# Weight sums of a seven-product feed-forward layer: from GpSimd to adding transfers and VectorE, with more blocks left at eight products

## The chip, the cores and the metric

The kernel runs on one core of a Trainium2 chip. The metric is the device time of one execution in microseconds (us), taken over several executions of the same program. The engines are named as in the profile: PE is TensorE (PEld its weight loads), DVE is VectorE, ACT is ScalarE, POOL is GpSimd, and SP is the engine whose queue issues nearly all transfers here. A transfer that POOL issues goes through the software queue; one that SP or ACT issues goes through a hardware queue.

## The reference, cut to what matters

The program computes one step of a two-layer transformer trunk for 512 latent tokens and 128 context tokens (640 columns in all) with a model width of 1024, all in float32. Layer 0 mixes with latent-attention and neighbourhood-attention heads, layer 1 with grouped-query attention. After each mixer stands a gated feed-forward layer of width 2816, and this is the part that the change touches:

```python
def swiglu(h, w_in, w_out):
    gate, up = jnp.split(h @ w_in, 2, axis=-1)
    return (jax.nn.silu(gate) * up) @ w_out
...
hp = modulate(rms_norm(xp, norm_ffn[l]), sh2_p, sc2_p)
hs = modulate(rms_norm(xs, norm_ffn[l]), sh2_s, sc2_s)
xp = xp + g2_p * swiglu(hp, w_ffn_in[l], w_ffn_out[l])
xs = xs + g2_s * swiglu(hs, w_ffn_in[l], w_ffn_out[l])
```

The shift, scale and gate vectors (sh, sc, g) of a layer are `silu(cond) @ w_mod[l] + b_mod[l]`, for two conditions. In layer 0 the last gate of layer 0 and five of the six vectors of layer 1 are still to be computed while the feed-forward layer runs; in layer 1 the last gate of layer 1.

## The kernel before, in words

**Precision.** Every float32 operand of a matmul is split into a rounded high part (ACT copies it, rounding) and a rest (one subtraction on DVE or POOL), and each product is three matmuls: high by high, high by rest, rest by high (`mm3`). Every matmul of the program is recorded at line 61, so stages are told apart by tile names.

**Input products of the feed-forward layer (`ffn`, L1026).** The width 2816 is cut into 22 blocks of 128. A block needs gate and up values: two weight tiles of 128 x 1024 (`wFI[l, fb, 0]` for gate and `[.., 1]` for up) against the activations of width 1024 and 640 columns, which are held as two halves of 320 columns. There are two ways to do a block.

- *Eight products* (`whole`, L1038; loop at L1067): gate and up, two column halves, eight slices of 128 of the width, three matmuls each, 96 matmuls of 320 columns. Only the two weight tiles have to be split (`unit`, L164). Blocks 0 and 1 of each layer go this way (`FEW = 2`, L1007).
- *Seven products* (loop at L1103, blocks 2 to 21): a Strassen-Winograd scheme over halves of the width, gate/up and column halves. It has seven products of four slices and three matmuls, 84 matmuls. Its left operands are the up tile itself (`wX`), half of the gate tile (`wW`), and four sums of halves of the two: two in `s13`, split into `wY`, two in `s24`, split into `wZ`. Before the change all four sums are made on POOL (L1117, L1118, L1121, L1122), each 128 x 512. Its right operands are four quadrants of the activations and the sums D, C, N, E of quadrants, made once per layer by `add_up` (L292); their rests for D and N are made on DVE, for C and E on POOL.

In a seven-product block PE's order is: X by quadrant 11, Y by D, the last product (W by E) of the block before, Z by N, X by 21, Z by 22, Y by C. Products that share a PSUM bank are taken out by ACT or DVE in between (`p1`, `p5`, `u1`, `g2`).

**Buffers.** Raw weight tiles come through a ring of three tiles (`rawp`, tag "raw", L159), which the up tiles, the tiles of the eight-product blocks and the modulation tiles `wm` share; the gate tiles have two of their own ("wr"). Split tiles have three places in each of two pools ("w"). `s13` and `s24` share two places ("ws"), taken in turn, so every `s13` takes the place of the `s13` before it. The outer ring has places for the results of a block (`hd`), which `hidden` (L1052) splits and sends to DRAM.

**Side work (`mod_side`, L1248).** While the blocks run, `step` feeds in the modulation product: for each 128 rows of `w_mod` one transfer of 512 KB into the raw ring and two DVE multiply-and-sum instructions (`junk`, L1265). How many after which block is written out by hand at L1285 to L1286 for layer 0 (48 tiles: 22 of them after the blocks from 5 on, one or two at a time, the rest in the output product) and at L1500 for layer 1 (8 tiles, one after each block from 2 on).

**Output product.** `wout` (L1163) loads and splits the output weights; its places alternate between the outer pools and a pool that opens when the block loop's pool closes.

**Order.** A scheduler sets the order of the instructions on each engine and of the transfers on each queue; every engine and every queue then works strictly in that order, so one that waits holds up what stands behind it. `ModS.make` (L276) makes the activation quadrants, partly on POOL (L286, L287), partly on DVE (L289, L290).

Of the kernel before, what the change touches and what calls it, by code (L numbers as in the profile page):

```python
# [18 lines left out]
P = 128  # L19
# [29 lines left out]
def body(ctx, tc, xT, vecs, crow, wm0, wm0g, wm1, wA, wNV, wNA, wMK, wMV, wOA, wGQ, wGK, wGV, wOC,  # L49
# [199 lines left out]
    class ModS:  # L249
# [26 lines left out]
        def make(self, i, rs, k):  # L276
            h, l = self.hl(k, i)
            c0, c1 = HALF[i]
            t = tp.tile([P, HT], F32, tag="u", bufs=7, name=f"{self.name}t{k}{i}")
            V.tensor_tensor(t, self.x[k][:, c0:c1], rs[:, c0:c1], ALU.mult)  # L280
            h32 = (self.left, self.right)[i][k]
            for a0, a1, c in HCOND[i]:
                self.act[k, i] = S.activation(h32[:, a0 - c0:a1 - c0], t[:, a0 - c0:a1 - c0], AF.Identity,
                                              bias=self.ml[:, self.sh + k, c:c + 1], scale=self.gsl[:, k, c:c + 1])
            if k % 2:
                G.tensor_scalar(h, h32, 1.0, 0.0, ALU.mult, ALU.add)  # L286
                G.tensor_tensor(l, h32, f(h), ALU.subtract)  # L287
            else:
                V.tensor_copy(h, h32)  # L289
                V.tensor_tensor(l, h32, f(h), ALU.subtract)  # L290

        def add_up(self, k):  # L292
            left = [self.left[j] for j in (k, k + 4)]
            b12, b22 = self.right[k], self.right[k + 4]
            n = tp.tile([P, HT], F32, tag="u", bufs=7, name=f"{self.name}n{k}")
            V.tensor_tensor(b22, b22, b12, ALU.subtract)
            V.scalar_tensor_tensor(n, b22, -1.0, left[0], ALU.mult, ALU.subtract)
            V.tensor_tensor(left[0], left[0], b12, ALU.subtract)
            V.scalar_tensor_tensor(left[1], n, -1.0, left[1], ALU.mult, ALU.subtract)
            for c, src in zip("DNCE", (left[0], n, b22, left[1])):  # L300
                t = self.sums[c][k]
                S.activation(t[:, 0:HT], src, AF.Copy)
                (V if c in "DN" else G).tensor_tensor(t[:, HT:T], src, f(t[:, 0:HT]), ALU.subtract)

    def residual(xo, xi, ps, ml, g, n, i):

# [697 lines left out]
                box["m"].make(c, nrm.rs, k)  # L1004
        return box, nxt

    FEW = 2  # L1007
    STAY = 3
    FIRST, SECOND = FO_ORDER[:9], FO_ORDER[9:]

# [15 lines left out]
    def ffn(l, x, pend, hm, nxt, side, opened):  # L1026
# [11 lines left out]
        def whole(ps, wt, k, c, first, last):  # L1038
            a, b = [w[:, k * P:k * P + P] for w in wt]
            mm3(ps[:, :HT], a, b, *hm.hl(k, c), first, last)  # L1040
# [23 lines left out]
                kept[fb] = dh, dl  # L1064

        step = None
        for fb in range(FEW):  # L1067
            pg, pu = [bank(f"fg{l}_{fb}{c}") for c in range(2)], pair(f"fu{l}_{fb}")
            g_, u_ = w1 if fb else w0
            for c in range(2):  # L1070
                for k in range(KT):
                    if fb == 0 and c == 0 and k == 3:
                        pend()
                        step = side(fk, hm.act[7, 1])
                        w1 = [after(hm.act[3 + 2 * i, 1], lambda: unit(wFI[l, 1, i], 1024, f"wgu{l}_1{i}")) for i in range(2)]
                        for j in range(4):
                            hm.add_up(j)
                    for ps, wt in ((pg, g_), (pu, u_)):
                        whole(ps[c], wt, k, c, k == 0, k == KT - 1)
            sg = tmp(f"sg{l}_{fb}")  # L1080
            for c, (c0, c1) in enumerate(HALF):
# [18 lines left out]
            step("fb", fb)  # L1100

        job = None
        for fb in range(FEW, FB):  # L1103

            ru = load(wFI[l, fb, 1], 1024, f"wu{l}_{fb}r")
            if fb == FEW:
                rg = load(wFI[l, fb, 0], 1024, f"wg{l}_{fb}r")
            else:
                rg = fp.tile([P, 1024], F32, tag="wr", bufs=2, name=f"wg{l}_{fb}r")
                nc.sync.dma_start(rg, wFI[l, fb, 0])  # L1110
# [3 lines left out]
            S.activation(wW[0], rg[:, 512:], AF.Copy)  # L1114
            V.tensor_tensor(wW[1], rg[:, 512:], f(wW[0]), ALU.subtract)
            s13 = fp.tile([P, 1024], F32, tag="ws", bufs=2, name=f"s13{l}_{fb}")
            G.tensor_tensor(s13[:, :512], rg[:, :512], rg[:, 512:], ALU.add)  # L1117
            G.tensor_tensor(s13[:, 512:], ru[:, :512], rg[:, :512], ALU.add)  # L1118
            wY = split(s13, f"wY{l}_{fb}")
            s24 = fp.tile([P, 1024], F32, tag="ws", bufs=2, name=f"s24{l}_{fb}")  # L1120
            G.tensor_tensor(s24[:, :512], s13[:, 512:], rg[:, 512:], ALU.add)  # L1121
            G.tensor_tensor(s24[:, 512:], s24[:, :512], ru[:, 512:], ALU.add)  # L1122
            wZ = split(s24, f"wZ{l}_{fb}")

            g, b5, b2 = bank(f"fg{l}_{fb}"), bank(f"fd{l}_{fb}"), bank(f"fu{l}_{fb}", "y")
# [37 lines left out]
        def wout(j0, n, tiles, name):  # L1163

            turn[0] += 1
            raw = (rawp.tile([P, 1024], F32, tag="raw", name=name + "r") if turn[0] % 2 else
                   fo.tile([P, 1024], F32, tag="raw", bufs=1, name=name + "r"))
# [3 lines left out]
            t = (wp.tile([P, 2, 1024], F32R, tag="w", bufs=3, name=name) if turn[0] % 2 else  # L1171
                 fo.tile([P, 2, 1024], F32R, tag="w", bufs=2, name=name))
# [102 lines left out]
    def x_again(n):  # L1275
# [7 lines left out]
    x, pend = mixer_out(wOA, oMs + oNs, [4, 5, 6, 7, 0, 1, 2, 3], x_again, mods[0], "oa", nxt, op[-1])  # L1283
    box2, nxt = next_mod("h10", gs[1][0], mods[1], SH1)
    side = mod_side([(0, wm0g, G2)] + [(1, wm1[j:j + 8], j) for j in (SH1, SC1, G1, SH2, SC2)],  # L1285
                    lambda kind, i: int(i > 4) + (i in (8, 11, 14, 17, 20)) if kind == "fb" else 1 + (i in (3, 5, 7)) if i < 8 else 2 + (i < 11) if i < 14 else 1)  # L1286
    x, pend = ffn(0, x, pend, box["m"], nxt, side, op)


# [368 lines left out]
```

## Time and profile before

| What | Value |
|---|---|
| Time, median of 3 runs | 1647.08 us (1644.03 to 1647.15) |
| The profiled execution: time | 1641.38 us |
| The profiled execution: span of the trace | 1639.6 us |
| TensorE clock granted, mean | 0.974 of full speed |
| Transfers | 212.65 MB, mean 130 GB/s |
| Software queue | 416 packets, 0.93 MB |

The span counts from the first to the last recorded instruction. In the profile's rows a group is given as line, engine, operation, output tile <- input tiles, shapes, and how many; buffer numbers are left out of the names, so that h01D in layer 0 is the tile of the sum D there, and h11D that of layer 1. A name in brackets after an idle time is what ended it. The first two rows of tenths in the page's second part tell which share of each fortieth of the span an engine was busy. The feed-forward layers lie at about 405 to 910 us and 1150 to 1632 us.

### The profile page before, as it was taken

What the parts mean: (1) busy time and instruction counts of PE and PEld (TensorE: products, weight loads), DVE (VectorE), ACT (ScalarE), POOL (GpSimd) and SP (SyncE); (2) the same over time, 40 slices, a digit from 0 to 9 for tenths busy, and PEclk for the clock granted to TensorE, in tenths of its full rate; (3) what the DMA queues carried; (4) which work ended last, traced back from release to release, by engine and by line L of the source; (5) the groups of instructions that cost most, each with busy time, mean ns of one, the idle gap of its engine ahead of it and who ended that gap; (6) DMA issues with size and microseconds to landing.
All of it is one profiled execution on the core that took longest, in us unless ns stands there. A gap on an engine that the chain in (4) does not pass through costs nothing.

```text
span 1639.6 us, 25446 instructions
## 1 busy us (share of the span) xinstructions
PE 1512.3 (92%) x9808; PEld 1434.6 (87%) x9808; DVE 1153.3 (70%) x1921; ACT 742.9 (45%) x1418; POOL 555.0 (34%) x498
## 2 busy tenths in 40 slices
PE   5999979999979888899999999999879999999997
PEld 3888858889868888889999989989868899999997
DVE  5656666875978898894895787784789867753333
ACT  4436566763544444342122556673544455541221
POOL 1225524522565455530000443222465555410000
PEclk9999979999979999999999999999999999999998
DMA  9334430004144544448863220002144443448311
GB/s 351 100 101 150 167 112 27 27 29 139 39 148 152 177 169 144 164 158 299 284 225 123 72 71 27 27 27 79 37 151 167 160 151 126 148 151 303 96 49 65
DMA packets 72970, 212.65 MB, mean 130 GB/s; under 512 B 8096, under 2 KB 12976, under 8 KB 72592
## 3 DMA queue, kind: packets, MB, share of 16 engines
q1 hardware_dynamic: 70080, 204.78, 36.7%
q10 hardware_dynamic: 2352, 5.31, 1.0%
q8 instruction: 77, 1.26, 0.3%
q0 software_dynamic: 416, 0.93, 0.2%
q14 instruction: 45, 0.37, 0.1%
HBM read 182.53 MB, written 28.46 MB: 129 GB/s over the span
## 4 chain that ended last, share of the span: by engine, by line
PE 56%; DVE 21%; DMA 10%; ACT 6%; issue 5%; POOL 2%; SPq 0%; ACTq 0%; DVEq 0%; POOLq 0%
PE fo L61 9%; PE fg L61 8%; DVE junk L1265 4%; DMA wm<-in_wm 4%; PE fd L61 3%; PE gq L61 2%; DMA wm<-in_wm0g 2%; DVE sg L1098 2%; PE nk L61 2%; PE nq L61 2%; PE fu L61 2%; DVE wX L1035 2%; PE mod L61 2%; PE go L61 1%; PE fo_2a L61 1%
## 5 line engine op out<-in xcount | busy, mean ns | idle before, releaser
L1265 DVE SCALAR_TENSOR_TENSOR junk<-wm,cb 128x1024 bf16<-128x1024 f32 x112 | 168.6, 1505 | 37.1 <-DMA wm<-in_wm 22.5
L1098 DVE TENSOR_TENSOR sg<-up,sg 128x640 f32<-128x640 f32 x40 | 62.1, 1553 | 49.0 <-ACT sg L1097 49.0
L61 PE MATMUL fg<-h01C,wY 128*128 128x320 f32 x240 | 43.7, 335 | 27.3 <-ACT u L1135 27.3
L61 PE MATMUL gq<-h10h,wgq 128*128 128x320 f32 x256 | 65.7, 315 | 0.2
L61 PEld LDWEIGHTS fg<-h01C,wY 128*128 128x128 f32 x240 | 38.5, 203 | 31.1 <-ACT u L1135 31.0
L244 POOL TENSOR_SCALAR h10h<-h10t,gs,mods 128x320 fp32r<-128x320 f32 x4 | 3.5, 876 | 182.8 <-DVE h10t L238 181.1
L1035 DVE TENSOR_TENSOR wY<-s,wY 128x1024 fp32r<-128x1024 f32 x40 | 60.3, 1507 | 1.8 <-ACT wY L1034 0.8
L1035 DVE TENSOR_TENSOR wZ<-s,wZ 128x1024 fp32r<-128x1024 f32 x40 | 50.5, 1263 | 7.6 <-ACT wZ L1034 7.6
L1034 ACT ACTIVATE wY<-s 128x1024 fp32r<-128x1024 f32 x40 | 42.4, 1059 | 22.5 <-PE fg L61 19.6
L1034 ACT ACTIVATE wZ<-s 128x1024 fp32r<-128x1024 f32 x40 | 42.1, 1053 | 20.0 <-PE fd L61 10.3
L61 PE MATMUL fg<-h11C,wY 128*128 128x320 f32 x240 | 41.2, 323 | 6.2 <-ACT u L1135 6.2
L61 PEld LDWEIGHTS gq<-h10h,wgq 128*128 128x128 f32 x256 | 44.7, 188 | 1.6 <-PE gtp L65 1.0
L61 PE MATMUL fg<-h01N,wZ 128*128 128x320 f32 x240 | 40.9, 322 | 5.4 <-ACT p L1129 5.4
L61 PE MATMUL fg<-h11N,wZ 128*128 128x320 f32 x240 | 40.1, 317 | 5.8 <-ACT p L1129 5.8
L61 PEld LDWEIGHTS fg<-h11C,wY 128*128 128x128 f32 x240 | 37.8, 197 | 7.4 <-ACT u L1135 7.4
L309 DVE SCALAR_TENSOR_TENSOR xr<-fo,mods,xr 128x320 f32<-128x320 f32 (+2 forms) x48 | 19.6, 436 | 35.0 <-PE fo L61 34.9
L61 PE MATMUL fd<-h01D,wY 128*128 128x320 f32 x240 | 40.0, 316 | 4.5 <-DVE wY L1035 4.5
L61 PE MATMUL fd<-h11D,wY 128*128 128x320 f32 x240 | 39.9, 316 | 4.5 <-DVE wY L1035 4.5
L61 PEld LDWEIGHTS fg<-h01N,wZ 128*128 128x128 f32 x240 | 37.9, 197 | 6.0 <-ACT p L1129 6.0
L61 PEld LDWEIGHTS fg<-h11N,wZ 128*128 128x128 f32 x240 | 37.4, 195 | 6.3 <-ACT p L1129 6.3
L61 PE MATMUL fg<-h01E,wW 128*128 128x320 f32 x240 | 39.0, 311 | 3.8 <-DVE g L1141 3.8
L61 PE MATMUL fg<-h01q,wX 128*128 128x320 f32 x240 | 41.9, 327 | 0.0
(3026 smaller groups left out, 5552.7 us busy)
## 6 DMA issues: line engine op xcount, KB each, us to landing
wm<-in_wm SPq DMA_DIRECT2D x48, 512.0 KB, 4.1
mraw<-in_wm SPq DMA_DIRECT2D x24, 512.0 KB, 3.9
mraw<-in_wm SPq DMA_DIRECT2D x8, 1024.0 KB, 15.3
wm<-in_wm0g SPq DMA_DIRECT2D x8, 512.0 KB, 4.5
x<-in_xT SPq DMA_DIRECT2D x8, 320.0 KB, 5.3
xr<-in_xT SPq DMA_DIRECT2D x8, 320.0 KB, 5.1
cb<-in_crow ACTq DMA_DIRECT2D x2, 1024.0 KB, 7.1
gt<-in_rpbp SPq DMA_DIRECT2D x8, 240.0 KB, 3.7
```

The costliest lines, as they stand in the source:

```text
L61: cls.last = nc.tensor.matmul(*a, **k)
L244: G.tensor_scalar(h[:, c0:c1], t, self.gsl[:, k, 0:1], self.ml[:, self.sh + k, 0:1], ALU.mult, ALU.add)
L309: V.scalar_tensor_tensor(xo[:, c0:c1], ps[:, c0 - o:c1 - o], ml[:, g + n, c:c + 1], xi[:, c0:c1], ALU.mult, ALU.add)
L1034: S.activation(t[:, 0, :], src, AF.Copy)
L1035: V.tensor_tensor(t[:, 1, :], src, f(t[:, 0, :]), ALU.subtract)
L1098: V.tensor_tensor(sg, up, sg, ALU.mult)
L1265: V.scalar_tensor_tensor(junk, raw, 1.0, cb[:, c, :], ALU.mult, ALU.mult, accum_out=mods[l][:, j0 + i, c:c + 1])
```

## The change

Five things change together.

- `FEW` becomes a pair: in layer 0 the first nine blocks, in layer 1 the first four keep eight products. Their weights from block 2 on are split by `unit` into the outer pool's three places.
- The sums: `s13` is filled by an SP transfer that reads the first half of the gate tile from DRAM twice, and then by two adding transfers of 128 x 512 that POOL issues, which add the second half of the gate tile and the first half of the up tile. The sums of `s24` go to DVE.
- The activations: for the second column half the rounding goes from POOL and DVE to ACT and all rests to DVE; all rests in `add_up` go to DVE, and the four calls of `add_up` stand behind blocks 0 and 1 (two each) instead of inside block 0.
- The side work of layer 0: none after blocks 0 to 2, then 3, 4, 3, 4, 3, 4 tiles after blocks 3 to 8, one after every third block from 9 on (five), then one after each of the first eight steps of the output product and two after the others.
- The first output weights (those over two tiles) always take the outer pools' places.

```diff
@@ ModS.make and add_up
-            if k % 2:
+            if i == 1:
+                S.activation(h, h32, AF.Copy)
+                V.tensor_tensor(l, h32, f(h), ALU.subtract)
+            elif k % 2:
...
-                (V if c in "DN" else G).tensor_tensor(t[:, HT:T], src, f(t[:, 0:HT]), ALU.subtract)
+                V.tensor_tensor(t[:, HT:T], src, f(t[:, 0:HT]), ALU.subtract)
@@ ffn
-    FEW = 2
+    FEW = 9, 4
...
+            if fb > 1:
+                g_, u_ = [unit(wFI[l, fb, i], 1024, f"wgu{l}_{fb}{i}") for i in range(2)]
+            else:
+                g_, u_ = w1 if fb else w0
...
-                        for j in range(4):
-                            hm.add_up(j)
...
+            if fb in (0, 1):
+                for j in (2 * fb, 2 * fb + 1):
+                    hm.add_up(j)
...
-            G.tensor_tensor(s13[:, :512], rg[:, :512], rg[:, 512:], ALU.add)
-            G.tensor_tensor(s13[:, 512:], ru[:, :512], rg[:, :512], ALU.add)
+            src = wFI[l, fb, 0][:, 0:512]
+            nc.sync.dma_start(s13.rearrange("p (a b) -> p a b", a=2),
+                              bass.AP(tensor=src.tensor, offset=src.offset, ap=[list(src.ap)[0], [0, 2], [1, 512]]))
+            nc.gpsimd.dma_start(s13[:, :512], wFI[l, fb, 0][:, 512:], accum_op=ALU.add)
+            nc.gpsimd.dma_start(s13[:, 512:], wFI[l, fb, 1][:, :512], accum_op=ALU.add)
...
-            G.tensor_tensor(s24[:, :512], s13[:, 512:], rg[:, 512:], ALU.add)
-            G.tensor_tensor(s24[:, 512:], s24[:, :512], ru[:, 512:], ALU.add)
+            V.tensor_tensor(s24[:, :512], s13[:, 512:], rg[:, 512:], ALU.add)
+            V.tensor_tensor(s24[:, 512:], s24[:, :512], ru[:, 512:], ALU.add)
@@ wout
+            early = len(tiles) > 1 or turn[0] % 2
@@ side work of layer 0
-                    lambda kind, i: int(i > 4) + (i in (8, 11, 14, 17, 20)) if kind == "fb" else 1 + (i in (3, 5, 7)) if i < 8 else 2 + (i < 11) if i < 14 else 1)
+                    lambda kind, i: (0, 0, 0, 3, 4, 3, 4, 3, 4)[i] if kind == "fb" and i < 9 else int(i % 3 == 0) if kind == "fb" else 1 if i < 8 else 2)
```

More of the change, by code (lines that the diff above doesn't have):

```diff
@@ L1066, in ffn @@
         step = None
-        for fb in range(FEW):
+        few = FEW[l]
+        for fb in range(few):
             pg, pu = [bank(f"fg{l}_{fb}{c}") for c in range(2)], pair(f"fu{l}_{fb}")
-            g_, u_ = w1 if fb else w0
+            if fb > 1:
+                g_, u_ = [unit(wFI[l, fb, i], 1024, f"wgu{l}_{fb}{i}") for i in range(2)]
+            else:
+                g_, u_ = w1 if fb else w0
             for c in range(2):
@@ L1102, in ffn @@
         job = None
-        for fb in range(FEW, FB):
+        for fb in range(few, FB):
             ru = load(wFI[l, fb, 1], 1024, f"wu{l}_{fb}r")
-            if fb == FEW:
+            if fb == few:
                 rg = load(wFI[l, fb, 0], 1024, f"wg{l}_{fb}r")
@@ L1165, in wout @@
             turn[0] += 1
-            raw = (rawp.tile([P, 1024], F32, tag="raw", name=name + "r") if turn[0] % 2 else
+            early = len(tiles) > 1 or turn[0] % 2
+            raw = (rawp.tile([P, 1024], F32, tag="raw", name=name + "r") if early else
                    fo.tile([P, 1024], F32, tag="raw", bufs=1, name=name + "r"))
@@ L1170, in wout @@
                               wFO[l, tiles[0]:tiles[0] + nt, :, j0 * P:(j0 + n) * P].rearrange("a p b -> p a b"))
-            t = (wp.tile([P, 2, 1024], F32R, tag="w", bufs=3, name=name) if turn[0] % 2 else
+            t = (wp.tile([P, 2, 1024], F32R, tag="w", bufs=3, name=name) if early else
                  fo.tile([P, 2, 1024], F32R, tag="w", bufs=2, name=name))
```

## The prediction

> **What bounds the kernel now.** I read the page's busy shares first, then the busy time by stretch, then PE's rows at the ends of the stretches, and last the waits of PE, DVE and the SP queue in the slow stretch.
>
> ```profile
> PE 1512.3 (92%) x9808; PEld 1434.6 (87%) x9808; DVE 1153.3 (70%) x1921; ACT 742.9 (45%) x1418; POOL 555.0 (34%) x498
> ...
> 404.70:451.50 46.80, 43.17 (x275) 40.32 (x274) 41.15 (x67) 25.84 (x53) 24.35 (x26) 1.00 0.11 34
> 451.50:754.10 302.60, 263.19 (x1670) 257.40 (x1669) 253.21 (x292) 128.25 (x207) 147.40 (x79) 0.94 0.48 163
> 1150.00:1198.20 48.20, 43.84 (x281) 41.29 (x281) 41.44 (x67) 27.96 (x55) 24.16 (x26) 1.00 0.11 33
> 1198.20:1470.80 272.60, 253.32 (x1671) 250.54 (x1670) 210.17 (x225) 131.13 (x205) 132.46 (x79) 0.97 0.44 149
> 1296.60:1469.00 172.40, 172.40 (x1178) 172.40 (x1177) 118.89 (x126) 88.52 (x138) 73.90 (x48) 1.00 0.40 137
> ```
>
> Behind each stretch stand its length, busy us of PE, PEld, DVE, ACT, POOL, the granted clock, the transfer share and GB/s. The second and fourth stretches are the twenty seven-product blocks of layers 0 and 1. The last, inside layer 1, has PE busy all through. So the same work is bound by PE late in layer 1 and by something else in layer 0, where PE idles while DVE is busy 84% of the time. The pace and the ends, from PE's rows in order of time:
>
> ```profile
> 451.52 1.92 PE L61 MATMUL fg<-h01q,wX 128*128 128x320 f32 x12
> 752.36 1.92 PE L61 MATMUL fg<-h01C,wY 128*128 128x320 f32 x12
> 1198.24 1.92 PE L61 MATMUL fg<-h11q,wX 128*128 128x320 f32 x12
> 1296.64 1.92 PE L61 MATMUL fg<-h11C,wY 128*128 128x320 f32 x12
> 1469.03 1.92 PE L61 MATMUL fg<-h11C,wY 128*128 128x320 f32 x12
> ```
>
> The last two rows are 14 blocks apart: 172.39 / 14 = 12.31 us for 84 matmuls, 0.1466 us each; twelve take 1.76. An eight-product block (96) then needs 14.07. Twenty blocks at PE's pace, to the end of the last C product, need 20 x 12.31 - 1.76 = 244.4. Layer 0 took 302.6 (752.36 + 1.76 - 451.52), layer 1 272.6: 58 and 28 us are lost. To what:
>
> ```profile
> PE fg L61 <- ACT u L1135: 27.3, 13, 3.6
> PE fg L61 <- ACT p L1129: 5.4, 2, 2.8
> PE fd L61 <- DVE wY L1035: 4.5, 1, 4.5
> ...
> DVE junk L1265 <- DMA wm<-in_wm: 19.3, 14, 3.2
> DVE junk L1265 <- DMA wm<-in_wm0g: 12.0, 7, 2.9
> ...
> SPq L161 <- DVE junk L1265: 78.0, 22, 4.5
> ...
> 551.40 2.44 PE L61 MATMUL fg<-h01C,wY 128*128 128x320 f32 x12 [3.58 <-ACT u L1135]
> 553.64 3.07 PE L61 MATMUL fg<-h01q,wX 128*128 128x320 f32 x12
> ```
>
> These are waits in layer 0's stretch (total, times, longest): PE waits for ACT's u, which stands behind DVE, which waits in order for the modulation tiles, whose transfers wait on SP until DVE frees a raw place. That is a ring of three tiles turning, 22 modulation tiles in it. After a wait of 3.58 us PE also runs slower: 551.40 to 556.55, where the next product starts, is 5.15 us instead of 3.52, that is 1.6 more.
>
> **The change, part by part.** The sum is made against the profiled execution, 1641.4 us (1639.6 of span); the median of the runs shown is 1647.1, 5.7 higher, which I add at the end.
>
> *More matmuls.* Seven blocks in layer 0 and two in layer 1 go from 84 to 96: 9 x 12 x 0.1466 = 15.8 us more PE work, all on the path. The floors become 7 x 14.07 + 13 x 12.31 - 1.76 = 256.8 in layer 0 and 2 x 14.07 + 18 x 12.31 - 1.76 = 248.0 in layer 1. Without any loss the change would gain 45.8 + 24.6 us; the rest of the working is what is lost again.
>
> *DVE and ACT rows for what follows:*
>
> ```profile
> 528.94 2.16 POOL L1122 TENSOR_TENSOR s<-s,wu_8r 128x512 f32<-128x512 f32 x1
> 529.98 2.19 DVE L1265 SCALAR_TENSOR_TENSOR junk<-wm,cb 128x1024 bf16<-128x1024 f32 x1
> 532.11 0.81 DVE L1098 TENSOR_TENSOR sg<-up,sg 128x640 f32<-128x640 f32 x1
> 532.85 0.68 DVE L1115 TENSOR_TENSOR wW<-wg_7r,wW 128x512 fp32r<-128x512 f32 x1
> 533.72 0.83 DVE L1056 TENSOR_TENSOR hd_2l<-sg,hd_2h 128x640 fp32r<-128x640 f32 x1 [0.20 <-ACT hd_2h L1055]
> 533.91 1.05 ACT L1034 ACTIVATE wX<-wu_8r 128x1024 fp32r<-128x1024 f32 x1
> 536.89 0.48 DVE L1137 TENSOR_TENSOR up<-fu,p 128x320 f32<-128x320 f32 x1
> 537.29 1.21 DVE L1265 SCALAR_TENSOR_TENSOR junk<-wm,cb 128x1024 bf16<-128x1024 f32 x1
> 541.50 1.22 DVE L1035 TENSOR_TENSOR wY<-s,wY 128x1024 fp32r<-128x1024 f32 x1
> 542.58 0.44 ACT L1097 ACTIVATE sg<-fg 128x320 f32<-128x320 f32 x1 [0.97 <-PE fg L61]
> ...
> wm<-in_wm SPq DMA_DIRECT2D x48, 512.0 KB, 4.1
> ...
> wu_2r<-in_wFI SPq DMA_DIRECT2D x2, 512.0 KB, 3.4
> ```
>
> The same DVE instruction takes 1.21 us alone and 2.19 beside a POOL sum. With POOL's sums gone I cost DVE by the short rows.
>
> *Layer 0, blocks 3 to 8, 21 modulation tiles.* DVE per block: two splits 2.4, two half products 1.0, the hidden rest 0.8, 3.5 tiles at 2 x 1.21 + 0.16 = 2.6 each 9.1: 13.3 of 14.07, no room for waits. The ring is worse. Per block 5.5 tiles pass three places. A modulation tile holds one for 4.1 (landing) + 2.6 + about 1 of queueing = 7.7; the gate tile for 4.1 + 1.05 + 1.22 + 1 = 7.4. The up tile's split place is free only when the block before has ended, so its raw tile is held about a block, 14.6. (3.5 x 7.7 + 7.4 + 14.6) / 3 = 16.3 us per block. PE then idles over 2 us per block, and some of the slow clock above comes with it, say 1.2: 17.5, or 3.5 lost per block, 21 in six. If the queueing hides completely, nothing is lost here (a rival below). The block boundary itself is covered: after a block's end ACT's silu 0.44, copy 1.05 and DVE's rest 1.22 are 2.7 us, and the gate products that stand ahead of the up products in PE's order (20 matmuls) take 2.9.
>
> *Sums by transfers.* Per seven-product block POOL's four sums go. In their place `s13` turns in a loop of its own, since every `s13` takes the place of the one before: SP's transfer (512 KB, 4.1) -> POOL's two adds -> ACT's copy 1.05 -> DVE's rest 1.22 -> SP again, with some 0.5 of semaphores. No row shows an add. The nearest is the software queue's 256 KB store, of the same size:
>
> ```profile
> L585 POOL DMA_DIRECT2D out_o_nv<-nvf x1: 607/607/607, 105.6 to 105.6; - x1
> ...
> DMA to landing us min/median/max: 3.2/3.2/3.2
> ```
>
> So the two adds land at least 0.6 + 3.2 = 3.8 us after POOL begins; a reason for less there is none. As upper end I take both landings doubled, one after the other, for reading the destination too, and 1.2 times for load (4.1 against 3.4 in the rows above): (0.6 + 6.4) x 1.2 = 8.4. I take 5.5, nearer the row, with load and a little for the reading. The loop is then 4.1 + 5.5 + 1.05 + 1.22 + 0.5 = 12.4 us against PE's 12.31: just level, 0.1 a block over 31 blocks, 3 us. The Trainium skill (DMA: Bandwidth & Descriptors, Rules for kernel authors) says that an adding transfer reads its destination and writes it later, and that one must wait for the earlier transfer's semaphore; that is why the legs of the loop follow each other here, and POOL's transfers do wait for SP's. The same page (Anatomy of one DMA) gives 2.0 us + bytes / 436,000 per us, an estimate of 2.6 us for 256 KB without adding; by it the loop would be 10.1 us and the 3 us fall away.
>
> *DVE in seven-product blocks.* Three splits 3.6, `wW` 0.7, the two sums of `s24` 1.4 (as `wW`), three drains 1.4, `sg` 0.8, hidden 0.8: 8.8 us of 12.31, 11.4 with a modulation tile. DVE now waits in order for the adds; behind that wait stands `g2`, which the closing product of the next block needs 3.5 us after the block's end, so about 3 us of lateness are free. In the blocks with a tile its 1.2 us also stand ahead of `wY` in the loop: 5 blocks in layer 0 and 6 in layer 1 at 1.2, 6 and 7 us.
>
> *Starts.* Before, the first Strassen block waited (4.5 for `wY`, 5.4 for p); now `add_up` and what stood there lie beside eight-product blocks. What is late next: DVE's eight more rests of 320 columns (0.48 each, about 4 us) ahead of block 2's weights, 2.5 us in layer 0, 3.5 with the later boundary in layer 1; and the entry into the seven-product blocks with DVE full, 4 us each (bounds 0 and the 10 lost there before).
>
> *Small gains.* Blocks 0 and 1 lose their POOL waits, a microsecond per layer; the early output weights another one. The output product keeps its order, with 22 modulation tiles instead of 26, hidden by PE's work there.
>
> *Sum.* Layer 0: 256.8 + 2.5 + 21 + 4 + 6 + 1 = 291.3, 11.3 less than 302.6. Layer 1: 248.0 + 3.5 + 4 + 7 + 2 = 264.5, 8.1 less than 272.6. With the 3 small ones 22.4: 1641.4 - 22.4 = 1619, and 1625 on the scale of the median.
>
> **Rivals.**
>
> 1. *The adds are slow (slower).* The loop of `s13` becomes the bound from the point where it exceeds 12.31. At 8.4 us for the two adds it is 15.3, 3.0 over, in 12 + 17 follow-on blocks, less 6 free: 81 us, in place of the 16 charged for loop and tiles: 1690. The gain is gone at about 1.5 us over, adds of 7.0 us. For: no row of an add, and the load rises, since some 1 MB per block joins the queues. Against: the 3.2 us row. 27%.
> 2. *The modulation tiles hide in the eight-product blocks.* Then 21 us come back: 1604. For: DVE's 13.3 fits in 14.07, and no POOL sum lengthens its rows. Against: the ring's 16.3. 15%.
> 3. *The ring does worse.* Twice the loss, 21 us a block, because SP's order holds other loads behind a waiting one: 1646, no change or slower. 10%.
>
> That the change does not do what it says is out: in the order of instructions POOL has only the two transfers left in each seven-product block.
>
> **How the numbers follow.** The forecast has 48%. 0.2% (3.3 us) is about what a measurement of this kernel can tell from no change. Faster: 46 of the forecast's 48 points, rival 2, one of rival 1: 62%. Same: 2 + 2 + 4 (rival 3): 8%. Slower: 24 + 6: 30%. The range reaches over rival 3 and most of rivals 1 and 2, to adds of about 8.1 us: 1602 to 1680.
>
> **What would show it.** After: seven-product blocks of layer 1 without tiles 12.3 us apart, else rival 1; then the adds land later than 7 us after POOL begins and DVE waits for them. Eight-product blocks 3 to 8 of layer 0 at 17 to 18 us with DVE waiting for `wm` and SP for DVE; at 14.1 it is rival 2. `junk` and `sg` rows in the blocks near 1.2 and 0.8 us. The prediction fails if adding costs far more than moving, or if DVE's rows do not shorten without POOL.

## The result and the profile after

The change makes the kernel slower: 1718.68 us (median of 4 runs, 1715.66 to 1723.22) against 1646.36 (4 runs of the kernel before, 1644.03 to 1647.15), a ratio of 1.0444 with a 95% interval of 1.0415 to 1.0473. The prediction was 1625 us with a range to 1680; the time lies above it, on the side of rival 1. The profiled execution took 1716.66 us (span 1714.9), 75.3 more than the one before.

The page of the kernel after: busy time, the software queue, and the chain of work that ended last, by engine and by line.

```profile
PE 1550.9 (90%) x9916; PEld 1468.2 (86%) x9916; DVE 1057.6 (62%) x1963; ACT 717.8 (42%) x1389; POOL 294.1 (17%) x368
...
q0 software_dynamic: 9344, 17.19, 5.7%
...
PE 48%; DMA 20%; DVE 18%; ACT 6%; issue 6%; POOL 1%; ACTq 0%; DVEq 0%; SPq 0%; POOLq 0%
DMA s<-in_wFI 14%; PE fo L61 9%; PE fg L61 3%; DVE junk L1277 2%; PE gq L61 2%; DMA wm<-in_wm 2%; PE nk L61 2%; DVE wX L1038 1%; PE nq L61 1%; PE go L61 1%; PE mod L61 1%; PE fo_2b L61 1%; PE fo_4b L61 1%; PE fo_2a L61 1%; PE fo_6b L61 1%
```

POOL's sums have turned into 9344 packets of the software queue (416 before). DVE and POOL are busy for less time than before, and yet the transfers into `s` alone are 14% of the chain. Where in the span that is, the busy time by stretch shows (length, then busy us of PE, PEld, DVE, ACT, POOL, the granted clock, transfer share, GB/s). The rows are the eight-product blocks 2 to 8 of layer 0, its thirteen seven-product blocks, blocks 2 and 3 of layer 1, and its eighteen seven-product blocks:

```profile
451.80:556.80 105.00, 100.21 (x668) 98.05 (x669) 79.06 (x121) 26.88 (x37) 0.00 (x0) 1.00 0.68 227
556.80:773.60 216.80, 179.32 (x1082) 174.17 (x1081) 124.92 (x177) 78.17 (x129) 21.34 (x24) 0.91 0.63 180
1218.40:1251.70 33.30, 29.47 (x189) 29.21 (x190) 19.90 (x28) 10.34 (x14) 1.80 (x2) 0.95 0.74 239
1251.70:1547.10 295.40, 244.68 (x1503) 238.86 (x1502) 157.91 (x214) 108.32 (x177) 28.45 (x32) 0.91 0.58 169
```

Layer 0 goes from 302.6 to 321.8 us, layer 1 from 272.6 to 328.7: 19.2 and 56.1 of the 75.3. The eight-product blocks are near PE's pace (105.0 for seven, floor 98.5). The seven-product blocks, counted as in the prediction with 1.76 us of overlap, take (216.8 + 1.8) / 13 = 16.8 and (295.4 + 1.8) / 18 = 16.5 us each, where PE needs 12.31. Three of the last C products of layer 1 in PE's rows, and then the waits between 1290 and 1545 us (total, times, longest):

```profile
1448.37 1.92 PE L61 MATMUL fg<-h11C,wY 128*128 128x320 f32 x12
1465.47 1.92 PE L61 MATMUL fg<-h11C,wY 128*128 128x320 f32 x12
1482.54 1.92 PE L61 MATMUL fg<-h11C,wY 128*128 128x320 f32 x12
```

```profile
DVE s L1132 <- DMA s<-in_wFI: 79.8, 14, 8.5
...
PE fg L61 <- DVE g L1152: 38.2, 12, 7.1
```

These blocks end 17.1 us apart. DVE stands 14 times, 79.8 us in all, at its first sum of `s24`, waiting for the adding transfers; PE waits for `g2` (12 times), which stands behind that sum in DVE's order. One whole turn of the loop in layer 1, from the timeline of all engines in order of time (the row of SP at 1475.91 starts the `s13` of block 19, the one at 1493.47 that of block 20):

```profile
1475.91 0.38 SPq L1126 DMA_DIRECT2D s<-in_wFI  x1
...
1479.39 0.33 SPq L1118 DMA_DIRECT2D wg_20r<-in_wFI  x1
...
1479.67 0.87 POOL L1128 DMA_DIRECT2D s<-in_wFI  x1 [15.28 <-DVE wW L1123]
1479.81 0.75 SPq L1064 DMA_DIRECT2D sp_16h<-hd_1h  x1
1480.25 1.20 POOL L1129 DMA_DIRECT2D s<-in_wFI  x1
1480.65 0.39 SPq L1064 DMA_DIRECT2D sp_16l<-hd_1l  x1
...
1488.20 0.69 DVE L1132 TENSOR_TENSOR s<-s,wg_19r 128x512 f32<-128x512 f32 x1 [6.74 <-DMA s<-in_wFI]
1488.81 1.22 DVE L1038 TENSOR_TENSOR wX<-wu_19r,wX 128x1024 fp32r<-128x1024 f32 x1
1489.95 0.48 DVE L1150 TENSOR_TENSOR up<-fd,u 128x320 f32<-128x320 f32 x1
1490.35 0.68 DVE L1133 TENSOR_TENSOR s<-s,wu_19r 128x512 f32<-128x512 f32 x1
...
1491.12 1.06 ACT L1037 ACTIVATE wZ<-s 128x1024 fp32r<-128x1024 f32 x1 [9.09 <-DVE s L1133]
...
1492.21 1.22 DVE L1038 TENSOR_TENSOR wZ<-s,wZ 128x1024 fp32r<-128x1024 f32 x1 [0.78 <-ACT wZ L1037]
...
1493.47 0.38 SPq L1126 DMA_DIRECT2D s<-in_wFI  x1
1493.52 1.22 DVE L1038 TENSOR_TENSOR wY<-s,wY 128x1024 fp32r<-128x1024 f32 x1
```

The turn has three legs: SP's transfer to the adds 3.76 us, the adds to DVE's first sum 8.53, from there to SP's next transfer 5.27; 17.56 together. The bracket of POOL's row names `wW`, which had just ended; what POOL waits for is the landing of SP's transfer, 3.20 us after its issue in this turn: POOL starts 0.5 to 0.6 us behind that landing in nearly every block.

SP starts 0.04 us after the end of DVE's rest of `wZ`, and DVE begins the rest of `wY` of the same block only then: the place that the next `s13` takes here is that of this block's `s24`. The last leg therefore holds both sums of `s24`, the rest of `wX` and a drain (`up`, a product taken out of PSUM) that stand between them in DVE's order, ACT's copy, and the rest of `wZ`.

The sentence in the section on the kernel before, that every `s13` takes the place of the `s13` before it, is thus not so: it can take either of the two places. In the changed kernel 29 of these transfers follow another one of their layer. Of them 16 start within 0.04 us of the end of the rest of `wZ`, 5 at the end of layer 0 and 11 in layer 1 after 1330 us. Twelve start as closely behind the rest of `wY` or the first sum of `s24`, the last readers of `s13`, and one behind another transfer of SP. Nor was it so in the kernel before, whose profile could have told. These are rows of DVE, POOL and DVE there:

```profile
1408.81 1.22 DVE L1035 TENSOR_TENSOR wZ<-s,wZ 128x1024 fp32r<-128x1024 f32 x1 [0.20 <-ACT wZ L1034]
...
1410.11 1.30 POOL L1117 TENSOR_TENSOR s<-wg_19r 128x512 f32<-128x512 f32 x1 [6.04 <-DVE wZ L1035]
1410.50 1.99 DVE L1035 TENSOR_TENSOR wY<-s,wY 128x1024 fp32r<-128x1024 f32 x1
```

POOL begins the `s13` of block 19 right behind the rest of `wZ` of block 18, and 0.39 us before DVE begins to read the `s13` of block 18 for `wY`.

Over the 27 turns that lie within a layer's blocks the three legs take 4.23, 8.16 and 4.25 us on average, 16.65 together (rounded), which is the length of the blocks above. Where `wZ` gives the place back (16 turns) they are 3.87, 8.43 and 5.27; in the other 11 they are 4.76, 7.77 and 2.78.

### The profile page after: what moved, and what is told of

The parts are those of the page before. It is cut to its first block, busy times and chain, and to the rows that moved or that the text cites. A ratio compares the mean times of both kernels' runs of the same rounds, so it can differ in the third digit from the quotient of the medians.

```text
span 1714.9 us, 25699 instructions
## 1 busy us (share of the span) xinstructions
PE 1550.9 (90%) x9916; PEld 1468.2 (86%) x9916; DVE 1057.6 (62%) x1963; ACT 717.8 (42%) x1389; POOL 294.1 (17%) x368
## 3 DMA queue, kind: packets, MB, share of 16 engines
q0 software_dynamic: 9344, 17.19, 5.7%
## 4 chain that ended last, share of the span: by engine, by line
PE 48%; DMA 20%; DVE 18%; ACT 6%; issue 6%; POOL 1%; ACTq 0%; DVEq 0%; SPq 0%; POOLq 0%
DMA s<-in_wFI 14%; PE fo L61 9%; PE fg L61 3%; DVE junk L1277 2%; PE gq L61 2%; DMA wm<-in_wm 2%; PE nk L61 2%; DVE wX L1038 1%; PE nq L61 1%; PE go L61 1%; PE mod L61 1%; PE fo_2b L61 1%; PE fo_4b L61 1%; PE fo_2a L61 1%; PE fo_6b L61 1%
## 5 line engine op out<-in xcount | busy, mean ns | idle before, releaser
L1277 DVE SCALAR_TENSOR_TENSOR junk<-wm,cb 128x1024 bf16<-128x1024 f32 x112 | 136.9, 1222 | 46.4 <-DMA wm<-in_wm 33.9
L1128 POOL DMA_DIRECT2D s<-in_wFI x31 | 27.2, 879 | 595.0 <-DMA s<-in_wFI 285.7
L61 PE MATMUL fg<-h11E,wW 128*128 128x320 f32 x216 | 49.4, 395 | 45.0 <-DVE g L1152 45.0
L61 PE MATMUL fg<-h01q,wgu 128*128 128x320 f32 x432 | 85.0, 313 | 0.9 <-DVE h01q L287 0.4
L61 PEld LDWEIGHTS fg<-h11E,wW 128*128 128x128 f32 x216 | 43.9, 254 | 48.8 <-DVE g L1152 48.7
L61 PEld LDWEIGHTS fg<-h01q,wgu 128*128 128x128 f32 x432 | 68.1, 188 | 3.6 <-DVE h01q L287 2.1
L61 PEld LDWEIGHTS fg<-h01E,wW 128*128 128x128 f32 x156 | 29.2, 234 | 24.5 <-DVE g L1152 24.5
L1038 DVE TENSOR_TENSOR wZ<-s,wZ 128x1024 fp32r<-128x1024 f32 x31 | 38.0, 1225 | 17.3 <-ACT wZ L1037 17.1
L61 PE MATMUL fg<-h11q,wgu 128*128 128x320 f32 x192 | 40.7, 321 | 0.9 <-DVE h11q L287 0.4
L1447 ACT ACTIVATE gp<-gs,gb,rq 128x640 f32<-128x640 f32 (+1 forms) x40 | 31.9, 797 | 19.8 <-DVE gb L1446 17.7
L61 PE MATMUL gq<-h10l,wgq 128*128 128x320 f32 x128 | 39.4, 308 | 0.0
```

What stands on the lines that cost most here:

```text
L61: cls.last = nc.tensor.matmul(*a, **k)
L1038: V.tensor_tensor(t[:, 1, :], src, f(t[:, 0, :]), ALU.subtract)
L1128: nc.gpsimd.dma_start(s13[:, :512], wFI[l, fb, 0][:, 512:], accum_op=ALU.add)
L1277: V.scalar_tensor_tensor(junk, raw, 1.0, cb[:, c, :], ALU.mult, ALU.mult, accum_out=mods[l][:, j0 + i, c:c + 1])
L1447: S.activation(dst, src, AF.Exp, bias=nb, scale=rq[:, j:j + 1], accum_out=ll[:, j:j + 1])
```

## The experiments

The theory after this reading: the whole loss is the loop of `s13`, set by its three legs one after the other. The rivals: the block split and the modulation plan lose too; DVE, now with the two sums, is itself the bound; the transfers' throughput sets the pace. All ratios are against the kernel before, run on the same chip.

**1. The sums back on POOL, the rest as changed.** (Here and in experiments 2 to 4 SP's transfer into `s13` goes or comes with the adds.)

```diff
-            nc.gpsimd.dma_start(s13[:, :512], wFI[l, fb, 0][:, 512:], accum_op=ALU.add)
-            nc.gpsimd.dma_start(s13[:, 512:], wFI[l, fb, 1][:, :512], accum_op=ALU.add)
+            G.tensor_tensor(s13[:, :512], rg[:, :512], rg[:, 512:], ALU.add)
+            G.tensor_tensor(s13[:, 512:], ru[:, :512], rg[:, :512], ALU.add)
...
-            V.tensor_tensor(s24[:, :512], s13[:, 512:], rg[:, 512:], ALU.add)
-            V.tensor_tensor(s24[:, 512:], s24[:, :512], ru[:, 512:], ALU.add)
+            G.tensor_tensor(s24[:, :512], s13[:, 512:], rg[:, 512:], ALU.add)
+            G.tensor_tensor(s24[:, 512:], s24[:, :512], ru[:, 512:], ALU.add)
```

> The four sums go back to POOL as before; the block split (nine and four eight-product blocks), the modulation plan and all else stay as changed. Theory: the loss lies in the loop of s13 alone (in late layer 1 one turn is 17.5 us: 3.8 from SP's transfer to the adds, 8.5 from the adds to DVE's sum, 5.3 from there to SP's next transfer), 31 blocks at about 16.6 instead of 12.3 to 13. Without it 1610 to 1630 us, late seven-product blocks of layer 1 12.3 us apart. Rival, the split or the modulation plan costs as well: at or above before, 1645 to 1680.

Measured: 1608.83 us, ratio 0.9765 (0.9749 to 0.9782). The split, the plan and the small edits gain 38 us by themselves; the sums are where the change loses.

**2. All four sums on DVE.**

```diff
-            nc.gpsimd.dma_start(s13[:, :512], wFI[l, fb, 0][:, 512:], accum_op=ALU.add)
-            nc.gpsimd.dma_start(s13[:, 512:], wFI[l, fb, 1][:, :512], accum_op=ALU.add)
+            V.tensor_tensor(s13[:, :512], rg[:, :512], rg[:, 512:], ALU.add)
+            V.tensor_tensor(s13[:, 512:], ru[:, :512], rg[:, :512], ALU.add)
```

> All four sums on DVE, no transfers for them; all else as changed. DVE per seven-product block: 8.8 us with two sums by the short rows, 10.2 with four, 12.8 in the blocks with a modulation tile (11 of 31). Theory (the loop of s13 is the loss): 1605 to 1630 us, late blocks of layer 1 12.3 us apart. Rival (DVE, or its order, is what makes the blocks long): still above 1660, blocks above 14 us.

Measured: 1580.60 us, ratio 0.9600 (0.9579 to 0.9622): 24 us below the lower end of the theory's range, and 28 below the sums on POOL. The stretches of the seven-product blocks of both layers (columns as above):

```profile
555.70:714.70 159.00, 158.70 (x1082) 158.35 (x1082) 140.34 (x203) 82.04 (x128) 0.00 (x0) 1.00 0.51 168
1190.00:1410.00 220.00, 220.00 (x1503) 220.00 (x1502) 176.13 (x246) 113.00 (x176) 0.00 (x0) 1.00 0.47 150
```

PE is busy all through, at full clock. DVE, with two sums more than in the changed kernel, is not the bound.

**3. POOL's `s13` as before, `s24` on DVE.** The DVE half of the edit alone.

```diff
-            nc.gpsimd.dma_start(s13[:, :512], wFI[l, fb, 0][:, 512:], accum_op=ALU.add)
-            nc.gpsimd.dma_start(s13[:, 512:], wFI[l, fb, 1][:, :512], accum_op=ALU.add)
+            G.tensor_tensor(s13[:, :512], rg[:, :512], rg[:, 512:], ALU.add)
+            G.tensor_tensor(s13[:, 512:], ru[:, :512], rg[:, :512], ALU.add)
```

> As changed, but s13 summed on POOL as before and only s24 on DVE. Theory (the DVE half of the change is harmless, the transfers alone lose): between the kernel with four sums on POOL (1609 us) and the one with four on DVE (1581 us), 1582 to 1605 us. Rival (DVE standing in order behind another engine's s13 is the harm): above 1612 us.

Measured: 1596.85 us, ratio 0.9692 (0.9676 to 0.9707). So the change comes apart, in this order of its parts, into 1646 -> 1609 (split, plan, small edits) -> 1597 (two sums to DVE) -> 1719 (the other two by transfers): -38, -12 and +122 us.

**4. The sums of the change in the kernel before.** Everything else as before: two eight-product blocks a layer, old plan.

```diff
-            G.tensor_tensor(s13[:, :512], rg[:, :512], rg[:, 512:], ALU.add)
-            G.tensor_tensor(s13[:, 512:], ru[:, :512], rg[:, :512], ALU.add)
+            nc.gpsimd.dma_start(s13[:, :512], wFI[l, fb, 0][:, 512:], accum_op=ALU.add)
+            nc.gpsimd.dma_start(s13[:, 512:], wFI[l, fb, 1][:, :512], accum_op=ALU.add)
...
-            G.tensor_tensor(s24[:, :512], s13[:, 512:], rg[:, 512:], ALU.add)
-            G.tensor_tensor(s24[:, 512:], s24[:, :512], ru[:, 512:], ALU.add)
+            V.tensor_tensor(s24[:, :512], s13[:, 512:], rg[:, 512:], ALU.add)
+            V.tensor_tensor(s24[:, 512:], s24[:, :512], ru[:, 512:], ALU.add)
```

> The kernel before with only its four sums replaced as in the change (two by adding transfers, two on DVE); two eight-product blocks per layer and the old modulation plan. Theory (the loop of s13 costs whatever the split): 40 blocks at 16 to 17 us, layer 0 about 332 instead of 303 us, layer 1 about 332 instead of 273: 1725 to 1745 us. Rival (the loss needs the new split or plan): within 15 us of before.

Measured: 1737.86 us, ratio 1.0551 (1.0530 to 1.0572). The loss needs neither the split nor the plan. Nor does it need the return by `wZ`: only one of these transfers starts right behind that rest here. The legs of the 36 turns within the layers are 5.52, 7.81 and 3.33 us on average, 16.67 together: SP's transfer and its landing take longer, the return is shorter, and the turn is as long.

**5. A second place for `s13`.** This breaks the loop and leaves every transfer as it is.

```diff
-            t = fp.tile([P, 2, 512], F32R, tag="w4", bufs=2, name=f"wW{l}_{fb}")
-            s13 = fp.tile([P, 1024], F32, tag="ws", bufs=2, name=f"s13{l}_{fb}")
-            s24 = fp.tile([P, 1024], F32, tag="ws", bufs=2, name=f"s24{l}_{fb}")
+            t = fp.tile([P, 2, 512], F32R, tag="w4", bufs=1, name=f"wW{l}_{fb}")
+            s13 = fp.tile([P, 1024], F32, tag="ws3", bufs=2, name=f"s13{l}_{fb}")
+            s24 = fp.tile([P, 1024], F32, tag="ws", bufs=1, name=f"s24{l}_{fb}")
```

> s13 gets two places of its own, s24 one, and wW one instead of two (to make room); the sums stay as changed. Theory: SP's transfer may then start a block earlier, so that one turn of the loop spans two blocks; the loop no longer binds, blocks 12.3 to 13.5 us apart, 1620 to 1650 us in all. Rival (the transfers' own throughput, or POOL's queue, sets the pace): blocks stay near 17 us, above 1700 us.

Measured: 1598.29 us, ratio 0.9699 (0.9663 to 0.9735), 120 us less than the change, and better than expected. The timeline of late layer 1:

```profile
1362.36 0.38 SPq L1126 DMA_DIRECT2D s<-in_wFI  x1
1367.36 0.88 POOL L1128 DMA_DIRECT2D s<-in_wFI  x1 [10.40 <-DMA s<-in_wFI]
...
1371.45 0.68 DVE L1132 TENSOR_TENSOR s<-s,wg_18r 128x512 f32<-128x512 f32 x1
...
1383.76 0.68 DVE L1132 TENSOR_TENSOR s<-s,wg_19r 128x512 f32<-128x512 f32 x1
```

DVE's sums no longer wait and stand 12.31 us apart. SP's transfer at 1362.36 follows the rest of `wY` of block 17, so it fills the `s13` of block 19, whose sum comes at 1383.76: 16.4 us after the adds began. The adds still land 7.0 us (median) after issue; they are as slow as before, only nobody waits. So the transfers' throughput is not the bound, the one place is. That `wW` gives up a place here is no rival for the gain: experiment 9 gives it up too and stays at 1710.60 us.

**6. The same transfers without adding.** This kernel leaves the additions out.

```diff
-            nc.gpsimd.dma_start(s13[:, :512], wFI[l, fb, 0][:, 512:], accum_op=ALU.add)
-            nc.gpsimd.dma_start(s13[:, 512:], wFI[l, fb, 1][:, :512], accum_op=ALU.add)
+            nc.gpsimd.dma_start(s13[:, :512], wFI[l, fb, 0][:, 512:])
+            nc.gpsimd.dma_start(s13[:, 512:], wFI[l, fb, 1][:, :512])
```

> POOL's two transfers move the same 256 KB to the same places without adding, so the additions are left out. What adding itself costs: if it is adding, the leg from the adds' issue to DVE's sum falls from 8.5 to about 4 us, the blocks to 13 us, the whole to about 1640 us; if it is the load of the other transfers or the queue of POOL, the leg stays at 7.5 to 8.5 us and the time within 15 us of 1718.

Measured: 1662.21 us, ratio 1.0084 (1.0052 to 1.0115). Neither end of what was expected: the leg falls, but by 2.1 us, not by 4. How POOL's transfers are issued and land, in the changed kernel by the page's groups and transfer issues, and here by the rows of the tile `s` on POOL (nanoseconds min/median/max of one issue):

```profile
L1128 POOL DMA_DIRECT2D s<-in_wFI x31 | 27.2, 879 | 595.0 <-DMA s<-in_wFI 285.7
...
s<-in_wFI POOLq DMA_DIRECT2D x62, 256.0 KB, 6.5
```

```profile
L1128 POOL DMA_DIRECT2D s<-in_wFI x31: 546/548/602, 351.7 to 1457.7; - x31
L1129 POOL DMA_DIRECT2D s<-in_wFI x31: 546/548/558, 352.3 to 1458.2; - x31
...
DMA to landing us min/median/max: 2.8/5.1/7.7
```

Adding makes the median landing 6.5 instead of 5.1 us, and POOL's row of the first issue 0.88 instead of 0.55. A transfer of 256 KB that adds nothing still takes 5.1 here, against the 3.2 of the row that the prediction leaned on, a store with nothing beside it; the least of the 62 took 2.8.

**7. The price with less beside it.** All four sums on DVE, and a chain of transfers into a scratch tile at the start of layer 1's attention, each line waiting for what it overwrites.

```diff
+    pt = gp.tile([P, 1024], F32, name="pt")
+    w0 = wFI[1, 0, 0]
+    nc.sync.dma_start(pt, w0)
+    nc.gpsimd.dma_start(pt[:, :512], w0[:, 512:], accum_op=ALU.add)
+    nc.gpsimd.dma_start(pt[:, :512], w0[:, 512:])
+    nc.gpsimd.dma_start(pt[:, :512], w0[:, 512:], accum_op=ALU.add)
+    nc.gpsimd.dma_start(pt[:, 512:], w0[:, :512], accum_op=ALU.add)
+    nc.gpsimd.dma_start(pt, w0)
+    nc.gpsimd.dma_start(pt, w0, accum_op=ALU.add)
+    nc.gpsimd.dma_start(pt[:, :256], w0[:, 512:768], accum_op=ALU.add)
+    nc.gpsimd.dma_start(pt[:, :256], w0[:, 512:768])
```

> All four sums on DVE, and in the quiet attention stage of layer 1 a chain of transfers on POOL's queue into a scratch tile, each after the one before has landed: 256 KB adding, 256 KB plain, 256 KB adding twice side by side, 512 KB plain, 512 KB adding, 128 KB adding, 128 KB plain. If adding itself is dear: 256 KB adding lands 1.5 us or more later than plain (about 5 against 3.2), two side by side at 5.5 to 6.5. If it is the load of other transfers: adding and plain within 0.3 us of each other, 3.2 to 3.5.

Issue to landing in us, from the rows of each line, one transfer each (the whole run took 1594.21 us, one time only; the diff leaves out the move of the sums to DVE):

| Size | adding | plain |
|---|---|---|
| 128 KB | 3.8 | 2.5 |
| 256 KB | 4.1 | 4.4 |
| 512 KB | 5.4 | 3.9 |

```profile
885.42 0.94 POOL L1393 DMA_DIRECT2D pt<-in_wFI  x1
...
886.89 1.26 POOL L1396 DMA_DIRECT2D pt<-in_wFI  x1
...
895.62 0.88 POOL L1395 DMA_DIRECT2D pt<-in_wFI  x1 [2.63 <-DMA pt<-in_wFI]
...
904.43 0.89 POOL L1398 DMA_DIRECT2D pt<-in_wFI  x1 [0.97 <-DMA pt<-in_wFI]
```

The scheduler put the second add of the intended pair (L1396) right behind the first of the chain (L1393), which took 5.3 and 5.1 us: 6.6 from the first's start to the second's landing. The stage was not empty (other loads ran beside these), and the 256 KB plain one, which began at 890.97 while the pair was still landing, is out of line. What stands, on one transfer of each kind: adding costs 1.3 to 1.5 us more at 128 and 512 KB; one 256 KB add alone lands after 4.1; a pair needs 6.6, where the changed kernel's took 8.3.

**8. One add of 512 KB instead of two of 256 KB.**

```diff
-            nc.gpsimd.dma_start(s13[:, :512], wFI[l, fb, 0][:, 512:], accum_op=ALU.add)
-            nc.gpsimd.dma_start(s13[:, 512:], wFI[l, fb, 1][:, :512], accum_op=ALU.add)
+            far = wFI[l, fb, 1][:, 0:512].offset - src.offset - 512
+            nc.gpsimd.dma_start(s13.rearrange("p (a b) -> p a b", a=2),
+                                bass.AP(tensor=src.tensor, offset=src.offset + 512, ap=[list(src.ap)[0], [far, 2], [1, 512]]), accum_op=ALU.add)
```

> As changed, but the two adding transfers of 256 KB of each s13 are one of 512 KB (two pieces of each row). In the quiet stage two adding transfers of 256 KB side by side took 6.6 us from the first one's start to the second's landing, one of 512 KB 5.4. Theory (the loop of s13 sets the block): the leg from the adds to DVE's sum falls by about 1.2 us and so does each of 31 blocks: 1675 to 1690 us. Rival (the other transfers set the landing): no gain, within 10 us of 1718.

Measured: 1723.54 us, ratio 1.0471 (1.0445 to 1.0497). No gain: the theory's size was wrong here and the rival's right. One adding transfer or two makes no difference under this load (legs in the table below).

**9. The gate tile's load out of the adds' way.**

```diff
...
-            rg = fp.tile([P, 1024], F32, tag="wr", bufs=2, name=f"wg{l}_{fb}r")
-            t = fp.tile([P, 2, 512], F32R, tag="w4", bufs=2, name=f"wW{l}_{fb}")
+            rg = fp.tile([P, 1024], F32, tag="wr", bufs=3, name=f"wg{l}_{fb}r")
+            t = fp.tile([P, 2, 512], F32R, tag="w4", bufs=1, name=f"wW{l}_{fb}")
```

> As changed, with three raw places for the gate tile instead of two (and one place for wW instead of two, for room): the gate tile's load of 512 KB need no longer wait for DVE's wW, so it starts right behind SP's transfer of s13 instead of beside the adds. Theory (the other transfers beside the adds, 512 KB of gate tile and 640 KB of spilled hidden tiles within 2 us of them, make 8.3 us of the quiet 5.4 to 6.6): the leg from the adds to DVE's sum falls by 1 us or more, while SP's leg of 3.8 us grows by up to as much; the block moves by -1.5 to 0 us, 1670 to 1718 us in all. Rival (the adds' own work under any load): the leg stays within 0.4 us of 8.3.

Measured: 1710.60 us, ratio 1.0386 (1.0358 to 1.0415). The legs of these four kernels, as differences of start times in the timeline like those read above, means over the turns of layer 1 after 1310 us whose last leg is 5.26 or 5.27:

| Kernel | turns | SP to adds | adds to DVE's sum | to SP again | turn |
|---|---|---|---|---|---|
| as changed | 11 | 3.84 | 8.29 | 5.27 | 17.40 |
| plain transfers (6) | 9 | 3.96 | 6.21 | 5.26 | 15.43 |
| one add (8) | 11 | 4.04 | 8.16 | 5.26 | 17.46 |
| gate load earlier (9) | 10 | 4.16 | 7.13 | 5.26 | 16.55 |

With the gate tile's 512 KB started 1.0 to 2.6 us before the adds in these turns, instead of 0.1 to 1.2 us, the leg falls by 1.16 us and the turn by 0.85. The time falls by only 8 us, since the turns of layer 0 do not follow (16.39 us on average as changed, 16.56 here). So of the 8.29 us some 2.1 are adding (6) and at least 1.2 the company of one load (9); the spilled tiles' 640 KB beside it were not tried alone, nor was DVE's work beside the adds.

**10. The kernel before with its four sums on DVE and nothing else.**

```diff
-            G.tensor_tensor(s13[:, :512], rg[:, :512], rg[:, 512:], ALU.add)
+            V.tensor_tensor(s13[:, :512], rg[:, :512], rg[:, 512:], ALU.add)
-            G.tensor_tensor(s13[:, 512:], ru[:, :512], rg[:, :512], ALU.add)
+            V.tensor_tensor(s13[:, 512:], ru[:, :512], rg[:, :512], ALU.add)
-            G.tensor_tensor(s24[:, :512], s13[:, 512:], rg[:, 512:], ALU.add)
+            V.tensor_tensor(s24[:, :512], s13[:, 512:], rg[:, 512:], ALU.add)
-            G.tensor_tensor(s24[:, 512:], s24[:, :512], ru[:, 512:], ALU.add)
+            V.tensor_tensor(s24[:, 512:], s24[:, :512], ru[:, 512:], ALU.add)
```

> The kernel before with its four sums on DVE instead of POOL and nothing else changed. DVE per block 10.2 us, with 22 modulation tiles in 20 blocks of layer 0 13.1, over PE's 12.3. Theory (POOL's sums cost through DVE's long rows and late drains; the split is worth little once they are gone): layer 0 262 to 275 us, layer 1 248 to 252, the whole 1580 to 1600 us. Rival (the eight-product blocks are what pays, since they hide the modulation tiles): 1610 us or more.

Measured: 1568.46 us, ratio 0.9526 (0.9512 to 0.9540), better than expected. Its seven-product blocks, layer 0 without the first, and layer 1 (columns as above):

```profile
467.10:700.70 233.60, 233.60 (x1595) 233.60 (x1595) 224.84 (x337) 121.42 (x189) 0.00 (x0) 1.00 0.59 190
1146.10:1395.60 249.50, 245.62 (x1670) 244.57 (x1669) 209.57 (x295) 129.97 (x201) 0.77 (x1) 1.00 0.49 162
```

PE is busy for all of 233.6 us although the modulation tiles lie there and DVE is busy 96% of it. Layer 0 took 302.6 us before, 58.2 over the floor of 244.4 for twenty seven-product blocks; here it takes 249.8, so that 5.4 are left without POOL's sums; the eight-product blocks, which cost 15.8 us of matmuls, are not needed.

**11. The changed kernel with four sums on DVE, two eight-product blocks a layer and the old plan.**

```diff
-    FEW = 9, 4
+    FEW = 2, 2
...
-                    lambda kind, i: (0, 0, 0, 3, 4, 3, 4, 3, 4)[i] if kind == "fb" and i < 9 else int(i % 3 == 0) if kind == "fb" else 1 if i < 8 else 2)
+                    lambda kind, i: int(i > 4) + (i in (8, 11, 14, 17, 20)) if kind == "fb" else 1 + (i in (3, 5, 7)) if i < 8 else 2 + (i < 11) if i < 14 else 1)
```

> The kernel as changed, with all four sums on DVE, two eight-product blocks in each layer and the old modulation plan: against the kernel before with its sums on DVE (1568 us) only the small edits of the change are left (second half of the operand and the sums' rests off POOL, add_up after its blocks, earlier output weights). Theory (the small edits are worth a microsecond or two each): 1560 to 1570 us. Rival (they cost, through DVE's eight more rests ahead of the first blocks): 1572 to 1580 us.

Measured: 1561.17 us, ratio 0.9487 (0.9466 to 0.9507): the best version found, 5.1% below the kernel before. The small edits are worth about 7 us over experiment 10 (different chips' runs, intervals just apart), and against experiment 2, which differs in split and plan alone, it is 19 us better: the split costs its 15.8 us of matmuls once nothing hides behind it.

## Why the prediction was wrong, step by step

**The step that failed is "Sums by transfers"**: the loop of `s13` at 4.1 + 5.5 + 1.05 + 1.22 + 0.5 = 12.4 us, charged 3 us over 31 blocks. It measured 4.23 + 8.16 + 4.25, 16.65 on average, and 3.84 + 8.29 + 5.27 = 17.40 in late layer 1. Two terms were mis-sized:

- *The adds*, taken at 5.5, took 8.2 to 8.3. They lay inside the bounds given (3.8 to 8.4), at the far end: some 2.1 us are adding (experiment 6) and at least 1.2 the company of one load (experiment 9); the rest over the row used was not split further. The value taken leaned on the nearest row, a store with nothing beside it, while the adds of late layer 1 start within some two microseconds of 1.15 MB of other transfers.
- *What follows the landing*, taken as ACT's copy, DVE's rest and semaphores, 2.8 us, took 4.25 on average. In the 11 turns that do not return by `wZ` the mean is 2.78, as said (single ones lie between 0.7 and 5.1, so that the agreement is partly luck). In the 16 that do it is 5.27, since DVE's order puts a sum, a rest, a drain and another sum ahead of the copy. The prediction said that DVE would wait in order for the adds and named `g2` behind that wait, but did not walk the whole return path in DVE's order, and took from the section on the kernel before that the place always comes back by `wY`. No bound was put on this term at all.

Experiments 1, 3 and 5 together show that the loop makes the loss: without the adding transfers it is gone, and a second place gives the whole 120 us back with the adds as slow as before.

**Rival 1 was the right mechanism, too small.** It put the adds at 8.4, about as measured, the loop at 15.3 and the time at 1690. The average turn is 1.35 us longer than 15.3, nearly all of it the return path. The seven-product blocks together took 134 us over their floor, against 24 charged for loop, tiles and entries: 110 more, and this alone would have given 1735.

**The eight-product blocks were costed too high.** Layer 0's seven took 105.0 us, 6.5 over the floor, where 2.5 + 21 were charged: rival 2's mechanism happened beside rival 1's and gave 17 us back. From 465 to 557 us these are the waits (total, times, longest) of DVE for modulation tiles and the two longest of PE for split weights, and the longest in total of SP's queue:

```profile
DVE junk L1277 <- DMA wm<-in_wm: 8.8, 4, 3.4
...
DVE junk L1277 <- DMA wm<-in_wm0g: 4.5, 4, 1.9
...
PE fu_3a L61 <- DVE wgu L170: 2.2, 1, 2.2
...
PE fu_7a L61 <- DVE wgu L170: 1.1, 1, 1.1
...
SPq L161 <- DVE junk L1277: 35.4, 16, 4.6
```

DVE waited 13.3 us for modulation tiles, PE at most 2.2 at a time for DVE's split weights. SP's queue still stood 35.4 us for DVE's `junk`, so the ring turns as described, but PE hardly notices. The blocks took 15.0 us each, and the ring's 16.3 was not reached; which of its holding times was too long was not measured by itself. Layer 1's two took 33.3 where 28.1 + 3.5 was said.

**What held.** PE's pace and the floors: PE's rows in experiments 2 and 10 stand 12.31 us apart. DVE's rows shorten without POOL's sums, `junk` to 1.22 us by this row of the page after:

```profile
L1277 DVE SCALAR_TENSOR_TENSOR junk<-wm,cb 128x1024 bf16<-128x1024 f32 x112 | 136.9, 1222 | 46.4 <-DMA wm<-in_wm 33.9
```

Starts and entries can't be told apart from the loop in the changed kernel. On the rule of the Trainium skill (DMA: Bandwidth & Descriptors, Rules for kernel authors) that an adding transfer reads its destination and must wait for the earlier one's semaphore, the trace agrees as to the order: POOL's adds start 3.8 us (mean of 11 turns) after SP's transfer, whose landing takes 3.3 (median), never ahead of it. The estimate that the prediction drew from the Trainium skill (DMA: Bandwidth & Descriptors, Anatomy of one DMA), 2.6 us for 256 KB, is near the least plain one here (2.8), but far from the medians of 5.1 us (plain) and 6.5 us (adding) under this kernel's load, and below the 4.1 of one add with less beside it.

The sum over the stretches closes: from the forecast's 1619 on the profiled scale, 110 for the seven-product blocks, less 17 and plus 2 for the eight-product ones, gives 1714, of 1716.66 measured.

## What to carry to other kernels

Where a buffer with one place is filled, changed and emptied by three engines, write out the whole turn until the place is free again, with every instruction that stands between in each engine's order, and take each transfer under the load that starts with it; a microsecond over the pace of the bound engine is paid in every block. Find out from the trace which reader really gives the place back. Here a second place was worth far more (120 us) than any speeding up of the legs that was tried. And before work is moved off a helper engine by a clever route, try the plain one: the four sums put on the busiest-looking helper, DVE, gave 4.7% with four letters changed.

## What the runs showed of the hardware that was not expected

- Work on POOL cost more than it saved (experiment 10 is 78 us faster without it): the four 128x512 sums took 1.3 to 2.3 us each there and lengthened DVE's rows beside them (1.21 to 2.19 us in the kernel before), while on DVE they take 0.68 each.
- DVE's durations overlap. Rows of 1.22 us start 1.14 apart and rows of 0.68 us 0.60 apart, so that a sum of durations overstates the load: the 13.1 us a block that experiment 10's expectation worked out from durations ran at 12.31. Two rows of experiment 10's timeline:

```profile
565.88 1.22 DVE L1035 TENSOR_TENSOR wZ<-s,wZ 128x1024 fp32r<-128x1024 f32 x1
567.02 1.22 DVE L1035 TENSOR_TENSOR wY<-s,wY 128x1024 fp32r<-128x1024 f32 x1
```

- The profile's row for the issue of an adding transfer on POOL is longer, 0.88 us for the first of a pair against 0.55 without adding, but POOL is not held for it: the second issue starts 0.58 us behind the first in the turn shown above, and 0.54 to 0.6 behind it in most pairs without adding.
